# Split weight tiles of the projections placed 64 bytes lower in SBUF

## The chip, the cores and the metric

The kernel runs on one core of one Trainium2 chip. The metric is the time of one execution on the device in microseconds, given as the median of several runs. The kernel before takes 1052.99 us (three runs, 1051.14 to 1053.38). A profile is one further execution, taken with the hardware profiler.

## What is computed

One encoder block over T = 1040 positions (16 meta tokens and 1024 of the sequence) with a model width of 1024. A normalised input goes through one wide projection; its parts feed a bidirectional retention branch (4 heads) and a windowed attention branch (8 query heads, 2 key groups); both are gated, projected, merged and projected again. Cut to what matters here:

```python
u = _rms_norm(h, pre_w)
z = u @ w_in
rq, rk, rv, rg, aq, ak, av, ag, gr, ga = _split_in(z)
...
o_r = _bidirectional_retention(rq, rk, rv, lg_f, lg_b)[:, META_PAD:]
y_r = (groupnorm(o_r) * ret_nw * silu(rg)) @ w_rb
o_a = _windowed_sink_attention(aq, ak, av, sink)[:, META_PAD:].reshape(B, T, ATT_Q)
y_a = (o_a * silu(ag)) @ w_ab
mix = sigmoid(gr) * y_r + sigmoid(ga) * y_a
return h + _rms_norm(mix @ w_o, post_w)
```

All of it is float32. The kernel splits each factor of a large product into a high and a low half and sums three matmuls for one product.

## The kernel before

**The product of halves.** `mm3` (line 74) issues three matmuls into one PSUM bank: high by high (line 76), low of the first factor by high of the second (line 77), high by low (line 78). The first argument is the stationary operand, which TensorE loads (128 columns, a row "PEld" in the profile), the second is the moving one, which it streams.

**The input.** `big` (line 133) holds the scaled input, high half in `big0`, low half in `big1`, as eight rows (k = 0 to 7) of 48 + 1040 columns. A row has 4352 bytes, 17 times 256. Position a begins at column 48 + a, so a block that begins at position 16 begins 256 bytes into the row.

**Projections.** A unit of weights is 1024 x 256. It is fetched to two raw tiles `wr` (line 105), and `halves_w` (line 112) splits each into a high tile `wh` (GpSimd or ScalarE) and a low tile `wl` (VectorE), of 128 x 1024 values, 4096 bytes a partition. There are four buffers of each in the pool `wp` (line 48).

- `proj` (line 136) has the weights stationary (128 columns of a `wh` or `wl` tile) and a block of `big` moving: 512 positions for retention's queries (tiles `pq`) and attention's queries (`paq`); 272, 256, 256 and 256 positions for retention's and attention's keys (`pk`, `pak`; `PIECES`, line 23).
- `projT` (line 157) has a block of 128 positions of `big` stationary and 256 columns of a weight tile moving (retention's values `pv`, attention's values `pav`). For the meta tokens the stationary operand is `xm` (48 or 16 columns), also in `wp`.
- `gen_pre` (line 796) computes parts of the gates' products ahead of time (tiles `pe`): weights `weh` and `wel`, again in the buffers of `wp`, stationary, and 512 positions of `big` moving.

**Order.** First a setup with the first head's queries and keys, then four heads of retention with the next projections filled in between (`retention`, line 446), attention's values (`gen_av`, line 872), attention (`attention`, line 1360) with the query projections and the `pe` pieces filled in between, and from 555 us on the gates, the two branch projections and the output projection in a form with seven products instead of eight (class `Phase`; tiles `bz`, `br`, `ba`, `bo`; its split weights are `lh`, `ll`). The order of work on each engine comes from the order of the program, from explicit "issue after" rules, and from a planner that simulates the program while it is built.

**Where the tiles lie.** The pools `edge`, `wp`, `aw` and later `lp` stand at the upper end of SBUF and grow downwards: a pool that needs more bytes begins at a lower address, and what stands below it moves down too. `edge` holds one tile (`nsink`). When attention is over, `wp` and `aw` are closed (line 1552) and `lp` takes their place directly below `edge` (line 1553). A tile of `lp` waits for the last use of those older tiles whose bytes it overlaps. In the program before the change, in bytes of a partition:

| tiles | pool | starts | start modulo 256 |
|---|---|---|---|
| `big`, blocks from position 16 on (256 bytes into a row) | keep | 7040 + multiples of 128 columns | 128 |
| `big`, the first piece of the keys (from position 0) | keep | 6976 | 64 |
| `wh` (four) | wp | 196480, 200576, 204672, 208768 | 128 |
| `wl` (four) | wp | 212864, 216960, 221056, 225152 | 128 |
| `xm` | wp | 194944 | 128 |
| `raw0`, `raw1` | aw | 175296, 176928 | 192, 32 |
| `aqh`, `aql` (attention's split queries, four each) | aw | 178560 to 192896, every 2048 | 128 |
| `kTh`, `kTl` (attention's keys, moving, blocks of 272 columns) | ra | 98432 on | 128, 192, 0, 64 |
| `vah` (attention's values, stationary) | va | 131328 on, every 1024 | 0 |
| `pah`, `pbh`, `Sh`, `kh` and the like | ap, rp | | 0 |
| `lh`, `ll` (split weights from 555 us on) | lp | 171904 to 194432, every 2048 | 128 |
| the two raw tiles of odd units, `wrz1_0` and `wrz1_1` | lp | 196480, 200576 | 128 |

`weh13` and `wel13`, the weights of the last `pe` pieces, lie in the buffers at 204672 and 221056; `weh11` lies at 200576.

The lines that the change touches: the two loops at line 273 in which the first `wh` and `wl` tiles are made, and `split_q` (line 645), which splits a block of attention's queries into `aqh` and `aql`.

Of the kernel before, what the change touches and what calls it, by code (L numbers as in the profile page):

```python
# [7 lines left out]
F32 = mybir.dt.float32  # L8
# [8 lines left out]
P = 128  # L17
# [22 lines left out]
def block_kernel(ctx: ExitStack, tc: tile.TileContext, x0, xT, x, meta, w_in, w_rb, w_ab, w_out, post_w,  # L40
# [7 lines left out]
    wp = w_stack.enter_context(tc.tile_pool(name="wp", bufs=1, side="right"))  # L48
# [42 lines left out]
    def dve_lo(o, i, hi):  # L91
        return nc.vector.tensor_tensor(o, i, hi.bitcast(F32), ALU.subtract).ins  # L92
# [174 lines left out]
    with tc.tile_pool(name="setup", bufs=1, reuse_waits="tile") as st:  # L267
# [6 lines left out]
        for i in range(2):  # L274
            raws.append(keep.tile([P, 4, 256], F32, tag="wr", bufs=2, name=f"wr0_{i}"))
            for j, lst in enumerate(wt):
                lst.append(wp.tile([P, 4, 256], R, tag="wl" if j else "wh", bufs=4, name=f"w0_{i}_{j}"))

        def w0_part(k0, k1):
            v = tuple(t[k0 // 4][:, k0 % 4:k0 % 4 + k1 - k0] for t in (raws, wt[0], wt[1]))  # L280
            nc.sync.dma_start(v[0], w_in[U_QK, :, k0:k1, :])
            if k0 == 4:
                nc.scalar.copy(v[1], v[0])
            else:
                raised[k0] = pool_hi(v[1], v[0])
            return lambda: dve_lo(v[2], v[0], v[1])
# [70 lines left out]
        for c in range(9):  # L357
            a, b = cols(c)
            t = st.tile([P, D if c < 7 else T], F32, tag="xn" if c < 7 else "xr", bufs=7 if c < 7 else KT - 1,
                        name=f"xn{c}")[:, 0:D]  # L360
# [282 lines left out]
    aq, aqs, wq = {}, {}, {}  # L643

    def split_q(hp, e_, i):

        o = aq[hp][e_, i]
        h, l = (aw.tile([P, 512], R, tag=f"aq{t}", bufs=4, name=f"aq{t}{hp}_{i}{e_}") for t in "hl")
        nc.scalar.copy(h, o)
        dve_lo(l, o, h)  # L650
        aqs[hp, e_, i] = h, l
# [702 lines left out]
    aw = w_stack.enter_context(tc.tile_pool(name="aw", bufs=1, reuse_waits="tile", side="right"))  # L1354
# [5 lines left out]
    def attention():  # L1360
# [4 lines left out]
        def stage1(hp, n):  # L1365
# [19 lines left out]
            for e_ in range(2):  # L1385
                hd = 2 * hp + e_
                if (hp, e_, i) not in aqs:
                    split_q(hp, e_, i)
                a_, b_ = (t[:, o0:o0 + P] for t in aqs[hp, e_, i])
                s = p2(f"ps{hd}_{n}")  # L1390
                mm3(s[:, 0:wid], a_, b_, kh[:, start:start + wid], kl[:, start:start + wid], True, True)
                if n == 0:
                    if hp:
                        raw[e_] = aw.tile([P, 401], F32, tag=f"raw{e_}", bufs=1, name=f"raw{hd}")
                    nc.vector.tensor_copy(raw[e_][:, 0:1], nsink[:, hd:hd + 1])
                p = pp[:, e_]
                nc.vector.tensor_tensor_reduce(raw[e_][:, 1:1 + wid], s[:, 0:wid], mask[0][:, mo:mo + wid], -SCALE,  # L1397
                                               nsink[:, hd:hd + 1], ALU.add, ALU.min, nm_[:, e_:e_ + 1])

                last["exp"] = nc.scalar.activation(p[:, 0:1 + wid], raw[e_][:, 0:1 + wid], AF.Exp, scale=-1.0,  # L1400
                                                   bias=nm_[:, e_:e_ + 1], accum_out=den[:, e_:e_ + 1]).ins
                pt.append(p[:, 1:401])
# [83 lines left out]
        for k, (hp, n) in enumerate(chunks):  # L1486
# [28 lines left out]
            if k in (12, 14, 21):  # L1515
# [3 lines left out]

    BEGUN = {0: [(fetch_aq, 1)], 9: [(half_w, 'q', 1, 0)], 10: [(sum_fetch, 0)], 12: [(half_w, 'q', 1, 1)],  # L1520
             14: [(pre_fetch, 7)], 17: [(split_q, 0, 0, 1)], 19: [(pre_sum, 7, 0)], 20: [(pre_sum, 7, 1)],
             21: [(split_q, 0, 1, 1)], 25: [(pre_sum, 7, 2)], 27: [(pre_parts, 7)], 28: [(pre_fetch, 8)],
             33: [(split_q, 1, 0, 0)], 34: [(sum_row, 0, 0)], 36: [(sum_row, 0, 1)], 38: [(split_q, 1, 1, 0)],
             39: [(sum_fetch, 1)], 40: [(pre_sum, 8, 0)], 41: [(pre_sum, 8, 1)], 42: [(pre_sum, 8, 2)],
# [129 lines left out]
```

## Time and profile before

| | us |
|---|---|
| median of three runs | 1052.99 |
| the profiled execution, whole | 1049.72 |
| its span, first to last instruction | 1047.6 |
| around the span | 2.12 |
| setup and the first head's queries and keys | 0 to 30 |
| retention with projections | 30 to 305 |
| attention's values | 305 to 335 |
| attention with query projections and `pe` pieces | 335 to 555 |
| gates (`bz`) | 555 to 812 |
| branch and output projections | 812 to 1047.6 |

In the profile, PE is TensorE's matmuls, PEld its loads of stationary operands, DVE is VectorE, ACT ScalarE, POOL GpSimd and SP the queue that issues most DMAs; "SPq" is such an issue. L76 is line 76. A row of matmuls gives the tiles as out<-moving,stationary or out<-stationary,moving with the buffer numbers left out, then the stationary and the moving shape. Matmuls overlap: the time from one start to the next is shorter than the duration of one, and where nothing stops them the two move together: a matmul that lasts some ns longer starts its successor as many ns later.

### The profile page before, as it was taken

The page shows a single profiled execution, that of the slowest core. Times are in us where ns is not written, and L with a number is a line of the kernel's source. Part 1 is how long each engine was busy: PE and PEld are TensorE (multiplying, and loading weights), DVE is VectorE, ACT ScalarE, POOL GpSimd, SP SyncE. Part 2 cuts the span into 40 slices and gives each one's busy share as a digit, 9 for nine tenths or more (in the row PEclk, how much of TensorE's full clock was granted, in tenths as well). Part 3 has the DMA queues.
Part 4 walks back from the last instruction along what each step waited for, and adds up shares of the span by engine and source line. Part 5 has one row for each costly group of instructions (what it writes and reads, how often), then busy time and mean ns, then how long its engine had stood idle before and what let it go on. Part 6 is the DMA issues. An engine that isn't in the chain of part 4 may idle for free. (4 is left out here: it accounts for less than half of the span.)

```text
span 1047.6 us, 17241 instructions
## 1 busy us (share of the span) xinstructions
PE 1032.9 (99%) x5880; PEld 906.8 (87%) x5880; DVE 838.9 (80%) x1788; ACT 505.6 (48%) x1127; POOL 227.1 (22%) x338
## 2 busy tenths in 40 slices
PE   8999999999999999999999999999999999999997
PEld 7998999989989888988888888787888788788886
DVE  6876768758876787777778988998899899877665
ACT  5541332522423557665667545455457446334443
POOL 3444244243342423443410000000000000111032
PEclk9999999999999999999999999999999999999999
DMA  9433123233341457665649579999935746789464
GB/s 352 165 85 88 61 45 88 75 71 109 82 99 62 100 153 200 182 168 136 186 153 350 193 255 333 298 328 348 379 131 169 242 171 217 233 224 330 131 121 80
DMA packets 98838, 188.43 MB, mean 180 GB/s; under 512 B 13024, under 2 KB 37632, under 8 KB 98192
## 3 DMA queue, kind: packets, MB, share of 16 engines
q1 hardware_dynamic: 81200, 162.89, 46.5%
q0 software_dynamic: 10176, 14.73, 9.4%
q10 hardware_dynamic: 7376, 9.73, 2.6%
q8 instruction: 46, 0.75, 0.3%
q14 instruction: 40, 0.33, 0.1%
HBM read 124.32 MB, written 57.68 MB: 174 GB/s over the span
## 5 line engine op out<-in xcount | busy, mean ns | idle before, releaser
L1269 POOL DMA_DIRECT2D mx_d<-c1a x4 | 3.6, 888 | 395.2 <-DVE c1a L1260 395.2
L77 PE MATMUL bz<-big,llz 128*128 128x512 f32 x192 | 74.8, 390 | 0.1
L76 PE MATMUL bz<-big,lhz 128*128 128x512 f32 x192 | 74.1, 390 | 0.5 <-ACT lhz L956 0.5
L78 PE MATMUL bz<-big,lhz 128*128 128x512 f32 x192 | 74.2, 389 | 0.0
L76 PE MATMUL pv<-wh,big 128*128 128x256 f32 x256 | 73.6, 288 | 0.0
L77 PE MATMUL pv<-wh,big 128*128 128x256 f32 x256 | 73.5, 287 | 0.0
L78 PE MATMUL pv<-wl,big 128*128 128x256 f32 x256 | 73.5, 287 | 0.0
L77 PE MATMUL bz<-T,llz 128*128 128x512 f32 x176 | 68.6, 390 | 1.1 <-DVE llz L92 1.1
L78 PE MATMUL bz<-T,lhz 128*128 128x512 f32 x176 | 68.5, 389 | 0.0
L76 PE MATMUL bz<-T,lhz 128*128 128x512 f32 x176 | 68.0, 389 | 0.0
L1400 ACT ACTIVATE p<-raw,nm 128x401 f32<-128x401 f32 (+1 forms) x64 | 38.3, 600 | 34.3 <-DVE nm L1397 33.0
L1410 POOL TENSOR_SCALAR p<-p,den 128x400 f32<-128x400 f32 (+1 forms) x60 | 37.7, 684 | 67.8 <-DVE den L1403 65.9
L76 PE MATMUL paq<-big,wh 128*128 128x512 f32 x128 | 51.4, 402 | 0.0
L77 PE MATMUL paq<-big,wl 128*128 128x512 f32 x128 | 50.0, 391 | 0.1
L78 PE MATMUL paq<-big,wh 128*128 128x512 f32 x128 | 50.1, 392 | 0.0
L76 PEld LDWEIGHTS pv<-wh,big 128*128 128x128 f32 x256 | 48.8, 191 | 0.4
L77 PEld LDWEIGHTS pv<-wh,big 128*128 128x128 f32 x256 | 48.8, 191 | 0.4
L78 PEld LDWEIGHTS pv<-wl,big 128*128 128x128 f32 x256 | 48.8, 191 | 0.3
L92 DVE TENSOR_TENSOR wl<-wr,wh 128x1024 fp32r<-128x1024 f32 x28 | 35.0, 1254 | 11.7 <-POOL wh L89 6.6
L76 PEld LDWEIGHTS bz<-big,lhz 128*128 128x128 f32 x192 | 36.0, 188 | 8.6 <-ACT lhz L956 1.3
L77 PEld LDWEIGHTS bz<-big,llz 128*128 128x128 f32 x192 | 36.0, 188 | 7.9 <-DVE llz L92 0.5
L78 PEld LDWEIGHTS bz<-big,lhz 128*128 128x128 f32 x192 | 36.0, 188 | 7.5
(616 smaller groups left out, 3598.5 us busy)
## 6 DMA issues: line engine op xcount, KB each, us to landing
wrz<-in_w_in_dram SPq DMA_DIRECT2D x32, 512.0 KB, 6.0
wr<-in_w_in_dram SPq DMA_DIRECT2D x29, 512.0 KB, 4.1
we<-in_w_in_dram SPq DMA_DIRECT2D x16, 512.0 KB, 4.3
tg<-tg_d SPq DMA_DIRECT2D x32, 256.0 KB, 5.1
e<-e ACTq DMA_DIRECT2D x20, 256.0 KB, 2.6
e<-e SPq DMA_DIRECT2D x20, 256.0 KB, 4.7
xn<-in_x_dram SPq DMA_DIRECT2D x8, 512.0 KB, 9.8
oTr_d<-ost SPq DMA_DIRECT2D x16, 256.0 KB, 2.1
```

Of the source, the lines that this page charges most:

```text
L76: nc.tensor.matmul(o, ah, bh, start=first, stop=False, **kw)
L77: nc.tensor.matmul(o, al, bh, start=False, stop=False, **kw)
L78: latest[:] = [nc.tensor.matmul(o, ah, bl, start=False, stop=last, **kw).ins]
L92: return nc.vector.tensor_tensor(o, i, hi.bitcast(F32), ALU.subtract).ins
L1269: nc.gpsimd.dma_start(d, to, accum_op=ALU.add)
L1400: last["exp"] = nc.scalar.activation(p[:, 0:1 + wid], raw[e_][:, 0:1 + wid], AF.Exp, scale=-1.0, bias=nm_[:, e_:e_ + 1], accum_out=den[:, ...
L1410: nc.gpsimd.tensor_scalar(pt[e_][:, 0:wid], pt[e_][:, 0:wid], den[:, e_:e_ + 1], 1.0, op0=ALU.mult, op1=ALU.mult)
```

## The change

Two tiles are allocated and never written or read: 64 bytes a partition in `wp`, after the first weight tiles, and 192 bytes in `aw`, after the first two query tiles. No instruction is added or removed.

```diff
@@ -275,6 +275,7 @@
             raws.append(keep.tile([P, 4, 256], F32, tag="wr", bufs=2, name=f"wr0_{i}"))
             for j, lst in enumerate(wt):
                 lst.append(wp.tile([P, 4, 256], R, tag="wl" if j else "wh", bufs=4, name=f"w0_{i}_{j}"))
+        wp.tile([P, 16], F32, name="space_w")
 
         def w0_part(k0, k1):
             v = tuple(t[k0 // 4][:, k0 % 4:k0 % 4 + k1 - k0] for t in (raws, wt[0], wt[1]))
@@ -646,6 +647,8 @@
 
         o = aq[hp][e_, i]
         h, l = (aw.tile([P, 512], R, tag=f"aq{t}", bufs=4, name=f"aq{t}{hp}_{i}{e_}") for t in "hl")
+        if not aqs:
+            aw.tile([P, 48], F32, name="space_aq")
         nc.scalar.copy(h, o)
         dve_lo(l, o, h)
         aqs[hp, e_, i] = h, l
```

With the two tiles at the upper ends of their pools, `xm`, `wh` and `wl` begin 64 bytes lower, at 64 modulo 256. The pool `aw` begins 64 + 192 = 256 bytes lower, so `raw0`, `raw1`, `aqh` and `aql` keep their place modulo 256. Everything else, `lp` included, keeps its address. Since `lp` stays and `wp` moves down, a tile of `lp` that ended where a tile of `wp` began now overlaps its first 64 bytes.

## The prediction

> **What bounds the kernel now.** I read the page's busy table first, then the same table by stretches of time.
>
> ```profile
> span 1047.6 us, 17241 instructions
> PE 1032.9 (99%) x5880; PEld 906.8 (87%) x5880; DVE 838.9 (80%) x1788; ACT 505.6 (48%) x1127; POOL 227.1 (22%) x338
> ...
> 30.00:85.00 55.00, 55.00 (x435) 53.38 (x433) 42.03 (x109) 22.48 (x62) 23.04 (x29) 1.00 0.32 94
> 335.00:555.00 220.00, 218.73 (x1292) 194.48 (x1290) 166.68 (x416) 134.98 (x354) 73.14 (x126) 1.00 0.58 161
> 555.00:806.00 251.00, 249.25 (x1100) 205.24 (x1100) 232.64 (x384) 141.32 (x252) 0.00 (x0) 1.00 0.81 279
> ...
> PE pq L76 <- ACT big L330: 1.6, 2, 1.1
> ```
>
> In a row of stretches stand the length, then busy time and count of PE, PEld, DVE, ACT and POOL. PE is busy in 55.00 of 55.00 us and in 218.73 of 220.00; the longest sum of waits of PE on any one line is 1.6 us (last row, from the list of waits). So the kernel is a train of matmuls without gaps, and the time is their number times their distance. The chain that ended last covers 0.4% of the span and says nothing more. What the change can do to the time it must do through the distance between matmuls that read a moved tile, or through a new wait that makes a gap.
>
> So the next view is the duration of such matmuls, by tile (minimum/median/maximum in ns) and by group (busy us, mean ns).
>
> ```profile
> L78 PE MATMUL bz<-big,lhz 128*128 128x512 f32 x192 | 74.2, 389 | 0.0
> L78 PE MATMUL paq<-big,wh 128*128 128x512 f32 x128 | 50.1, 392 | 0.0
> L77 PE MATMUL paq<-big,wl 128*128 128x512 f32 x128 | 50.0, 391 | 0.1
> L78 PE MATMUL pe<-big,weh 128*128 128x512 f32 x80 | 31.3, 392 | 0.0
> L78 PE MATMUL pq<-big,wh 128*128 128x512 f32 x48 | 18.7, 390 | 0.0
> ...
> L78 PE MATMUL paq<-big,wh x128: 387/389/398, 293.3 to 504.1; 128*128 128x512 f32 x128
> L77 PE MATMUL pq<-big,w x16: 389/395/398, 5.7 to 27.0; 128*128 128x512 f32 x16
> ```
>
> A matmul of 512 columns has a settled duration, 389 ns: it is the median everywhere, and the mean too in the gates, where one follows the other undisturbed. And it has an unsettled one, around 395: the median in the setup, where matmuls of 512, 272 and 256 columns alternate. The projections between retention and attention pieces lie between, at 390 to 392. The cause of the unsettled ones shows where a row of settled matmuls ends.
>
> ```profile
> L78 PE MATMUL paq<-big,wh x3: 389/389/396, 436.6 to 438.0; 128*128 128x512 f32 x3
> 437.96 0.40 PE L78 MATMUL paq<-big,wh 128*128 128x512 f32 x1
> 438.20 0.28 PE L76 MATMUL po<-pah,vah 128*128 128x256 f32 x1
> ...
> L78 PE MATMUL paq<-big,wh x2: 389/389/389, 442.7 to 443.4; 128*128 128x512 f32 x2
> 443.42 0.39 PE L78 MATMUL paq<-big,wh 128*128 128x512 f32 x1
> 443.64 0.28 PE L76 MATMUL pak<-big,wh 128*128 128x256 f32 x1
> ```
>
> Both are the last of a settled row, and both are followed by one of 256 columns, whose stationary operand is loaded while they stream. At 437.96 that operand is `vah`, which begins at 0 modulo 256, and the matmul takes 396 ns; at 443.42 it is a `wh` tile, at 128 like the block of `big` that streams, and it takes 389. So what the next load reads seems to matter to a stream by some 7 ns, and the place modulo 256 is what I see differ. All 512-wide work in this kernel has both at 128. The change takes that equality away from all projections.
>
> **The change part by part.** Nothing is removed or issued anew; three things move.
>
> *(a) The 512-wide projections* (`pq`, `paq`, `pe`): stationary at 64, moving at 128. By the counts, (128 + 80 + 48) x 3 = 768 matmuls; the 48 of the setup, unsettled already, are not in it. The trace has no 512-wide stream beside a load 64 bytes off, so I bound it: from below by the fastest of the row of `paq`, 387 ns, from above by the slowest, 398. Against the present mean of about 391.5 (392, 391, 392, 390 in the rows above) that is -3.5 to +5 us over 768. I take 395, the unsettled median: 768 x 3.5 ns = +2.7 us.
>
> *(b) The 256-wide ones* (`pv`, `pav`, `pk`, `pak`). Here the weights are moving at 64 and `big` stationary at 128, or the reverse.
>
> ```profile
> L78 PE MATMUL pk<-big,wh 128*128 128x256 f32 x72 | 20.3, 282 | 0.0
> L78 PE MATMUL pk<-big,wh 128*128 128x272 f32 x24 | 6.9, 288 | 0.0
> L78 PE MATMUL pv<-wl,big x256: 277/283/385, 31.0 to 275.8; 128*128 128x256 f32 x128
> L78 PE MATMUL pav<-wl,big x64: 279/283/364, 308.4 to 334.9; 128*128 128x256 f32 x64
> L78 PE MATMUL pak<-big,wh 128*128 128x256 f32 x48 | 13.5, 282 | 0.0
> L76 PE MATMUL pb<-Shb,qh 128*128 128x256 f32 x4 | 1.1, 280 | 0.0
> L77 PE MATMUL pb<-Shb,ql 128*128 128x256 f32 x4 | 1.1, 281 | 0.0
> ```
>
> There are (256 + 64 + 72 + 48) x 3 = 1320. Their settled duration is 283 ns, and the unsettled one is the shorter: `pb` (groups of a window, 85 to 108 us), three matmuls at a time between other work, has 280 to 281. The 272-wide pieces of the keys are the only long rows that have the two operands 64 bytes apart already (moving at 64, stationary at 128). Between 283 ns at 256 columns and 389 at 512 a column costs (389 - 283) / 256 = 0.41 ns, so 272 settled ones would take 289.6; they take 288. Both rows say 1.5 to 2.5 ns less. Bounds: from 278 (near the minima, 277 and 279) to 285 (the mean of L76 of `pk`, stalls included) against 283, so -6.6 to +2.6 us. I take -1.5 ns: 1320 x 1.5 = -2.0 us.
>
> ```profile
> L76 PE MATMUL pk<-big,wh 128*128 128x256 f32 x72 | 20.5, 285 | 0.0
> ```
>
> The 272-wide ones, (24 + 16) x 3 + 24 = 144, get both operands to 64 and may settle: +1.6 ns each, +0.2 us. The meta matmuls (stationary `xm`, moving `wh`, both in `wp`) keep their distance: nothing.
>
> *(c) The new overlap in `lp`.* Of the tiles that overlap 64 bytes of a further weight tile, one meets a late one: `wrz1_1` now ends inside `weh13`, and its load has to wait for the last `pe` matmul. Three others that matter early (`wrz1_0`, `llz1_1`, the first `xT`) get `weh11`, `weh10` and `wel11`, whose pieces come before those of `weh13` and are through when the first of these loads is issued.
>
> ```profile
> 544.96 4.35 SPq L1200 DMA_DIRECT2D wrz<-in_w_in_dram  x4
> 549.36 16.26 SPq L1120 DMA_DIRECT2D xT<-xs  x15
> ...
> 553.38 0.69 DVE L994 TENSOR_TENSOR stz0S<-wrz,wrz 128x512 f32<-128x512 f32 x1 [3.30 <-PE pe L78]
> 558.47 0.68 DVE L994 TENSOR_TENSOR stz1S<-wrz,wrz 128x512 f32<-128x512 f32 x1
> DMA to landing us min/median/max: 3.7/5.3/6.7
> ...
> 554.93 0.40 PE L76 MATMUL bz<-big,lhz 128*128 128x512 f32 x1
> 558.77 0.62 ACT L932 CAST big<-xT 128x512 fp32r<-128x512 f32 x1
> 563.88 0.68 DVE L92 TENSOR_TENSOR llz<-stz1S,lhz 128x512 fp32r<-128x512 f32 x1
> 564.39 0.84 PE L76 MATMUL bz<-big,lhz 128*128 128x512 f32 x3
> ```
>
> The four loads `wrz` are issued from 544.96 to 549.31, `wrz1_1` last. The last `pe` matmul ends at 553.38, where DVE is released. So the load is issued some 4.4 us later, and the fifteen `xT` loads behind it on SP's queue with it. With the landing times of the third row from the end of that block (3.7 to 6.7 us) it is there at 557.1 to 560.1; its first reader is DVE at 558.47, so DVE comes 0 to 1.6 us late, and everything queued behind that instruction on DVE with it, up to the split of 563.88 that the matmuls of 564.39 want. The three L76 in one row there show that PE takes the high parts first because the low one is just being made: there is little slack. The `xT` loads are first read at 558.77 by ACT; issued at 553.8 they may come as late, but PE needs those products only after 570 us: six others of 12 matmuls come first, from 554.93 on, at some 0.227 us a matmul, the 0.22 to 0.24 us between the starts in the rows at 438 and 443. Bounds 0 to +1.6 us; DVE's other splits can go on meanwhile, so I take +0.5. The planner may put another load in front instead; the same bounds hold.
>
> *(d) The splits themselves.*
>
> ```profile
> L92 DVE TENSOR_TENSOR wl<-wr,wh x28: 1186/1224/1660, 24.7 to 465.8; 128x1024 fp32r<-128x1024 f32 x28
> ```
>
> DVE now reads `wr` at 128 and `wh` at 64. The work stands beside PE's full stretches above and is prepared well ahead; if one took 16 ns more, 28 would be 0.4 us on an engine that is not the bound. Zero. Attention's queries keep their place: zero.
>
> The sum: 2.7 - 2.0 + 0.2 + 0.5 = +1.4 us. Made against the profiled execution, 1049.72 becomes 1051.1; the runs shown stand 3.3 us above it, so 1052.99 becomes 1054.4.
>
> The Trainium skill speaks against (a) and (b): "TensorE: Matmul & The Clock Gate", Part 2, Step-by-step, says that TensorE has two independent SBUF read ports, one for the streaming operand and one for the load, and that a load takes no read bandwidth from the running matmul. By it (a) and (b) would be nothing and the sum +0.5 us. The rows of 437.96 and 443.42 (396 against 389 ns) do not agree with it to the last 7 ns, so I give it a rival's place only (the third below).
>
> **The rivals.**
>
> *Only the 512-wide pay (slower).* One mechanism: stream and load collide in every matmul as at 437.96, and the 256-wide ones stay at 283 because they find another settled rhythm. Price: (397 - 391.5) x 768 = +4.2, with (c) +4.7 us: 1057.7. It decides from a 512-wide mean of about 394.5 on, where (a) alone passes 2.1 us. For it: the step to 396 with a load 128 bytes off. Against it: the 272-wide rows, 64 bytes off, are not slow.
>
> *The collisions get fewer (faster).* If 64 bytes between the two is better than none, as the 272-wide rows hint, the 256-wide gain 3 ns (283 to 280, the `pb` row) and the 512-wide lose their restarts (391.5 to 389.5): -4.0 - 1.5 + 0.5 = -5.0 us at best; I put it at -3.5: 1049.5. Against it: at 512 columns the unsettled state is the longer one.
>
> *Places don't matter to TensorE.* The 7 ns come from something else that differs between `po` and `pak`. For it: the skill's rule, and the score matmuls, whose moving operand begins at 0, 64 or 128 bytes from the stationary one with no row standing out. Then only (c) is left: 1053.5.
>
> ```profile
> L76 PE MATMUL ps<-kTh,aqh 128*128 128x400 f32 x48 | 16.6, 345 | 0.0
> L77 PE MATMUL ps<-kTh,aql 128*128 128x400 f32 x48 | 16.5, 344 | 0.0
> ```
>
> **How the numbers follow.** Forecast 0.34, only the 512-wide 0.29, fewer collisions 0.21, no influence 0.16. A measurement of this kernel tells about 0.2% (2.1 us) from no change. The forecast's own range is 1052.5 to 1056.5; it is slower by more than 2.1 us in four cases of ten. Slower: 0.14 + 0.28 + 0.01 = 0.43; faster: 0.19 from the third case and 0.02 from the others; the same: 0.36. The range reaches from the faster case to somewhat above the slower one, 1049.3 to 1059; the ends where all bounds of (a) and (b) meet are left out.
>
> **What would show it.** (a): medians of `paq`, `pe` and `pq` at 394 to 397 instead of 389, with `bz` still at 389. (b): medians of `pv`, `pav`, `pk` at 280 to 282. The 272-wide at 289 to 290. (c): the fourth `wrz` load issued after 553 us and a gap of PE below 1.6 us near 564. The forecast is wrong if the 512-wide rows stay at 389, if the 256-wide go above 284, or if the time moves by more than PE's durations and the gap of (c) add up to.

## The result, and the profile after

The changed kernel takes 1047.56 us (median of 8 runs, 1046.44 to 1050.19), the kernel before beside it 1051.82 us (8 runs, 1050.68 to 1053.38). The ratio is 0.9965, with a 95% interval of 0.9956 to 0.9974: faster by 0.35%, where 1054.4 us was forecast and the range ended at 1049.3 us. The profiled execution took 1046.49 us against 1049.72, so the pair of traces below shows 3.2 us of the 4.3 us between the medians; the rest can't be traced in them.

First the page of the changed kernel: span and busy times.

```profile
span 1044.4 us, 17239 instructions
PE 1029.6 (99%) x5880; PEld 902.3 (86%) x5880; DVE 838.4 (80%) x1788; ACT 506.2 (48%) x1127; POOL 227.8 (22%) x338
```

The span is 3.2 us shorter and PE is busy for 3.3 us less (1032.9 before) with the same 5880 matmuls; PE's idle time stands as before, at 14.8 us against 14.7. So no wait went away: the matmuls themselves stand closer. Which ones shows in the busy time of one tile's matmuls over the whole span. In such a row stand the stretch, its length, PE's busy time and matmul count, PEld's, then the engines that read the tile; the last three numbers are the clock, the DMA share and GB/s. Overlapping matmuls are counted once, so in a row without gaps this is the count times the distance from start to start. The kernel before, in the order `pv`, `pav`, `pk`, `pak`, `paq`, `pe`, `pq`, `bz`:

```profile
0.00:1060.00 1060.00, 117.58 (x832) 104.78 (x832) 14.76 (x36) 13.24 (x36) 1.00 0.58 178
0.00:1060.00 1060.00, 27.71 (x208) 25.60 (x208) 4.21 (x9) 4.16 (x9) 1.00 0.58 178
0.00:1060.00 1060.00, 55.18 (x384) 50.99 (x384) 14.27 (x36) 1.00 0.58 178
0.00:1060.00 1060.00, 27.20 (x192) 24.73 (x192) 6.21 (x16) 1.00 0.58 178
0.00:1060.00 1060.00, 93.86 (x384) 70.42 (x384) 20.57 (x32) 1.00 0.58 178
0.00:1060.00 1060.00, 58.77 (x240) 44.13 (x240) 11.68 (x20) 1.00 0.58 178
0.00:1060.00 1060.00, 48.24 (x192) 34.50 (x192) 11.81 (x18) 1.00 0.58 178
0.00:1060.00 1060.00, 252.40 (x1104) 206.77 (x1104) 42.04 (x62) 23.36 (x40) 1.00 0.58 178
```

The changed kernel, the same tiles in the same order:

```profile
0.00:1060.00 1060.00, 114.99 (x832) 102.59 (x832) 14.77 (x36) 13.27 (x36) 1.00 0.58 178
0.00:1060.00 1060.00, 26.79 (x208) 24.79 (x208) 4.21 (x9) 4.17 (x9) 1.00 0.58 178
0.00:1060.00 1060.00, 54.80 (x384) 50.60 (x384) 14.28 (x36) 1.00 0.58 178
0.00:1060.00 1060.00, 26.89 (x192) 24.43 (x192) 6.18 (x16) 1.00 0.58 178
0.00:1060.00 1060.00, 94.18 (x384) 70.42 (x384) 20.56 (x32) 1.00 0.58 178
0.00:1060.00 1060.00, 58.98 (x240) 44.12 (x240) 11.66 (x20) 1.00 0.58 178
0.00:1060.00 1060.00, 48.35 (x192) 34.43 (x192) 11.81 (x18) 1.00 0.58 178
0.00:1060.00 1060.00, 253.02 (x1104) 206.75 (x1104) 42.06 (x62) 23.32 (x40) 1.00 0.58 178
```

Where the weights stream (`pv`, `pav`) PE is busy 2.59 + 0.92 us less; where they are loaded and 256 or 272 columns of `big` stream (`pk`, `pak`) 0.38 + 0.31 us less; where 512 columns of `big` stream (`paq`, `pe`, `pq`) 0.32 + 0.21 + 0.11 us more. Together that is -4.20 + 0.64 = -3.56 us. The gates take 0.62 us more, though none of their operands moved and their distance from start to start is 226.8 ns in both kernels. A second profile of the changed kernel (from its repeated run, the last but one of the experiments) has 252.67 us there, 0.27 us more than before, so part of it is scatter; the experiment on the overlap returns to the rest.

The durations by tile (minimum/median/maximum in ns) of the changed kernel:

```profile
L78 PE MATMUL pv<-wl,big x256: 275/278/384, 30.7 to 272.7; 128*128 128x256 f32 x128
L78 PE MATMUL pav<-wl,big x64: 276/276/367, 305.2 to 330.8; 128*128 128x256 f32 x64
L78 PE MATMUL paq<-big,wh x128: 388/394/405, 290.1 to 499.6; 128*128 128x512 f32 x128
L78 PE MATMUL bz<-big,lhz x192: 389/389/397, 551.3 to 808.7; 128*128 128x512 f32 x192
```

The medians of `pv` and `pav` fell from 283 to 278 and 276 ns. That of `paq` in this row (L78) rose from 389 to 394, as step (a) said it would, and yet `paq` costs only 0.32 us more: a median of durations does not say how far apart the starts are, and 393 was its mean where 392 was before.

### The profile page after: what moved, and what is told of

Same layout as the page of the kernel before. It is cut to its first block, busy times and chain, and to the rows that moved or that the text cites. A ratio compares the mean times of both kernels' runs of the same rounds, so it can differ in the third digit from the quotient of the medians.

```text
span 1044.4 us, 17239 instructions
## 1 busy us (share of the span) xinstructions
PE 1029.6 (99%) x5880; PEld 902.3 (86%) x5880; DVE 838.4 (80%) x1788; ACT 506.2 (48%) x1127; POOL 227.8 (22%) x338
## 5 line engine op out<-in xcount | busy, mean ns | idle before, releaser
L77 PE MATMUL bz<-big,llz 128*128 128x512 f32 x192 | 74.8, 390 | 0.1
L78 PE MATMUL bz<-big,lhz 128*128 128x512 f32 x192 | 74.2, 389 | 0.0
L77 PE MATMUL pv<-wh,big 128*128 128x256 f32 x256 | 72.7, 284 | 0.0
L78 PE MATMUL pv<-wl,big 128*128 128x256 f32 x256 | 72.6, 284 | 0.0
L77 PE MATMUL bz<-T,llz 128*128 128x512 f32 x176 | 68.6, 390 | 0.5 <-DVE llz L92 0.5
L78 PE MATMUL bz<-T,lhz 128*128 128x512 f32 x176 | 68.5, 389 | 0.0
L78 PE MATMUL paq<-big,wh 128*128 128x512 f32 x128 | 50.3, 393 | 0.0
L77 PE MATMUL paq<-big,wl 128*128 128x512 f32 x128 | 50.2, 392 | 0.1
L77 PEld LDWEIGHTS pv<-wh,big 128*128 128x128 f32 x256 | 48.2, 188 | 0.4
L78 PEld LDWEIGHTS pv<-wl,big 128*128 128x128 f32 x256 | 48.3, 188 | 0.3
L77 PEld LDWEIGHTS bz<-big,llz 128*128 128x128 f32 x192 | 36.0, 188 | 7.9 <-DVE llz L92 0.5
L78 PEld LDWEIGHTS bz<-big,lhz 128*128 128x128 f32 x192 | 36.0, 188 | 7.5
```

The source lines that it names most:

```text
L77: nc.tensor.matmul(o, al, bh, start=False, stop=False, **kw)
L78: latest[:] = [nc.tensor.matmul(o, ah, bl, start=False, stop=last, **kw).ins]
```

## The experiments

In all of them "distance" is the place of the streamed operand minus that of the operand loaded beside it, modulo 256. In the changed kernel it is -64 for `pv` and `pav` (weights stream at 64, `big` is loaded at 128) and +64 for `pk`, `pak`, `paq`, `pe` and `pq` (`big` streams at 128, weights are loaded at 64). Each ratio is against the kernel before in runs on the same chip, whose median was 1051.0 to 1051.4 us.

### The distance: four places of the weights

Queries moved along with the weights (the tile in `aw` left out):

```diff
-        if not aqs:
-            aw.tile([P, 48], F32, name="space_aq")
```

> Weights at 64 modulo 256 as in the changed kernel, but attention's queries are not kept: aqh and aql begin at 64 too. Theory (the distance modulo 256 between the operand that streams and the one that is loaded beside it sets a matmul's duration): only the score matmuls ps change their distances, and they come three at a time; at most 0.3 us either way, 1047.3 to 1048.0. Rival (the queries have to stay at 128): the ps rows rise from 344 or 345 ns to 348 or more, at least +0.5 us and some more through longer restarts behind them, 1048.5 to 1050.

Measured: 1047.28 us, ratio 0.9967 (0.9954 to 0.9979). That is the changed kernel: keeping the queries at 128 plays no part in it.

Weights at 0, 128 bytes from `big`:

```diff
-        wp.tile([P, 16], F32, name="space_w")
+        wp.tile([P, 32], F32, name="space_w")
-            aw.tile([P, 48], F32, name="space_aq")
+            aw.tile([P, 32], F32, name="space_aq")
```

> Weights at 0 modulo 256, 128 bytes from the blocks of big; queries still at 128. Theory of the distance: the 512-wide projections stay at 394 to 397 ns as in the one matmul at 437.96 of the kernel before, some +2 us against the changed kernel; the 256-wide ones lie anywhere between 277 and 283. Time 1048.5 to 1052. Rival (an odd multiple of 64 bytes as the tiles' own place is what helps): 0 is as 128, pv and pav back at 283 and the 512-wide at 389, 1051.8 as before.

Measured: 1053.0 us, ratio 1.002 (1.001 to 1.0029).

Weights at 192, which exchanges the two signs:

```diff
-        wp.tile([P, 16], F32, name="space_w")
+        wp.tile([P, 48], F32, name="space_w")
-            aw.tile([P, 48], F32, name="space_aq")
+            aw.tile([P, 16], F32, name="space_aq")
```

> Weights at 192 modulo 256, again 64 bytes from big, on the other side; queries at 128. Theory of the distance with a sign: what pv and pav gained (weights streaming, 64 before big) now goes to pk and pak (big streaming, 64 before the weights), and pv and pav get what pk and pak had: pv and pav near 281 ns, pk and pak near 278 or 279; since pv and pav are 960 of the 1320, about 1 to 1.5 us slower than the changed kernel, 1048.5 to 1049.5. Rival (own place, odd multiple of 64): as the changed kernel in every row, 1047.6.

Measured: 1051.63 us, ratio 1.0007 (0.9994 to 1.002).

Weights a full 256 bytes lower, at 128 again, as a control on everything else that moves with the pool:

```diff
-        wp.tile([P, 16], F32, name="space_w")
+        wp.tile([P, 64], F32, name="space_w")
-        if not aqs:
-            aw.tile([P, 48], F32, name="space_aq")
```

> Weights 256 bytes lower, so at 128 modulo 256 again, queries too; the pools move further than in the changed kernel, and wrz1_1 overlaps weh13 by 256 bytes. Theory of the distance: every row of the projections as before the change (512-wide 389, 256-wide 283, paq L78 392), 1051.8. Rival (any move of the pool, or the new overlap in lp, made the gain): as the changed kernel, 1047.6.

Measured: 1051.17 us, ratio 1.0 (0.9988 to 1.0012).

The control's rows of busy time, `pv` and `paq`:

```profile
0.00:1060.00 1060.00, 117.59 (x832) 104.80 (x832) 14.81 (x36) 13.24 (x36) 1.00 0.59 178
0.00:1060.00 1060.00, 93.90 (x384) 70.42 (x384) 20.58 (x32) 1.00 0.59 178
```

The same with the weights at 0:

```profile
0.00:1060.00 1060.00, 117.03 (x832) 104.18 (x832) 14.84 (x36) 13.24 (x36) 1.00 0.59 178
0.00:1060.00 1060.00, 95.24 (x384) 70.56 (x384) 20.58 (x32) 1.00 0.59 178
```

And with the weights at 192, `pv`, `pk` and `paq`:

```profile
0.00:1060.00 1060.00, 116.27 (x832) 103.56 (x832) 14.81 (x36) 13.24 (x36) 1.00 0.59 178
0.00:1060.00 1060.00, 54.18 (x384) 50.21 (x384) 14.29 (x36) 1.00 0.59 178
0.00:1060.00 1060.00, 95.47 (x384) 70.43 (x384) 20.58 (x32) 1.00 0.59 178
```

A move by 256 changes nothing: to 0.04 us the rows of `pv` and `paq` are those of before. So the place modulo 256 decides, and not the order of the tiles or the overlaps. At 128 bytes the 512-wide pay (`paq` +1.38 us) and the 256-wide gain little (`pv` -0.55). At 192 the signs are exchanged, and so are the gains: `pk`, now at -64, gains 1.00 us where the changed kernel gave it 0.38, `pv`, now at +64, gains 1.31 instead of 2.59, and `paq`, now at -64, pays 1.61 instead of 0.32. The whole comes out at no change that the runs can tell. Both times missed what was expected: 1053.0 us against 1048.5 to 1052 with the weights at 0, and 1051.63 us against 1048.5 to 1049.5 at 192, where only the 256-wide matmuls had been thought to exchange their gains and the price of the 512-wide at -64 was left out.

### Distance or place: both operands moved

Weights at 192 and everything on the left side of SBUF, `big` among it, 64 bytes higher, at 192 too:

```diff
-    mhalf = keep.tile([P, 40], F32, name="mhalf")
+    mhalf = keep.tile([P, 56], F32, name="mhalf")
-        wp.tile([P, 16], F32, name="space_w")
+        wp.tile([P, 48], F32, name="space_w")
-            aw.tile([P, 48], F32, name="space_aq")
+            aw.tile([P, 16], F32, name="space_aq")
```

> Weights at 192 modulo 256 as in the third experiment, and everything on the left side of SBUF 64 bytes higher, so that big stands at 192 too. The stream and the loads of the projections are then at distance 0 as before the change; in the gates, branches and output (2100 matmuls of 512 columns) the stream stands 64 bytes above the loaded operand, which keeps 128. Theory of the signed distance: pv back at 119.2 ns from start to start, pk at 119.3, paq and pe at 228.7; bz, br, ba, bo +0.8 ns on 226.7, that is +1.7 us; in all 1053. Rival, the weights' own place: pv 117.4, pk 115.4, paq and pe 233 as in the third experiment, the gates unchanged: 1051.6.

Measured: 1052.21 us, ratio 1.0011 (1.0002 to 1.002). `pv`, `paq` and `bz`:

```profile
0.00:1060.00 1060.00, 117.59 (x832) 104.79 (x832) 14.81 (x36) 13.28 (x36) 1.00 0.59 178
0.00:1060.00 1060.00, 93.89 (x384) 70.43 (x384) 20.58 (x32) 1.00 0.59 178
0.00:1060.00 1060.00, 254.54 (x1104) 207.04 (x1104) 42.49 (x62) 23.39 (x40) 1.00 0.59 178
```

Weights left where the change put them (64), and the left side 64 bytes lower, so that `big` stands at 64:

```diff
-    mhalf = keep.tile([P, 40], F32, name="mhalf")
+    mhalf = keep.tile([P, 24], F32, name="mhalf")
```

> The changed kernel (weights at 64 modulo 256) with everything on the left side of SBUF 64 bytes lower, so that big stands at 64 as well: distance 0 in the projections, and in the 2100 matmuls of the gates, branches and output the stream 64 bytes below the loaded operand. Theory of the signed distance (third experiment: 512-wide 233 ns with the stream 64 below): pv, pav at 119.2, paq, pe at 228.7, and bz, br, ba, bo up to 4 to 6 ns longer than 226.7, that is +8 to +13 us: 1060 to 1065. Rival, the weights' own place: pv 115.7 as in the changed kernel, gates 226.7, time 1047.6. Rival, distance without sign: gates +0.8 ns, 1053.

Measured: 1058.77 us, ratio 1.0071 (1.0055 to 1.0087). `pv`, `paq` and `bz`:

```profile
0.00:1060.00 1060.00, 117.58 (x832) 104.78 (x832) 14.82 (x36) 13.28 (x36) 1.00 0.59 178
0.00:1060.00 1060.00, 93.93 (x384) 70.42 (x384) 20.58 (x32) 1.00 0.59 178
0.00:1060.00 1060.00, 259.17 (x1104) 207.25 (x1104) 42.53 (x62) 23.40 (x40) 1.00 0.59 178
```

Its page:

```profile
span 1056.2 us, 17239 instructions
PE 1044.5 (99%) x5880; PEld 907.0 (86%) x5880; DVE 838.6 (79%) x1788; ACT 507.2 (48%) x1127; POOL 228.9 (22%) x338
```

In both kernels the weights are moved and the distance is 0, and `pv` and `paq` are back at 117.6 and 93.9 us, the rows of before. The weights' own place is thereby ruled out. The gates, which the change left alone, now feel it: at +64 `bz` is busy for 2.14 us more than before, at -64 for 6.77 us more. The sizes were less well foreseen. At +64 the gates' distance grew by 2.1 ns, not 0.8 (from 226.8 to 228.9, in the table below), which over 2100 matmuls would be 4.4 us, and the time rose by some 1.2 us (the ratio), with PE 3.0 us longer busy and 1.5 us less idle in the profile; at -64 it grew by 6.5 ns, and PE was busy for 11.6 us more (1044.5 against 1032.9) while the span grew by 8.6, since PE's idle time shrank from 14.7 to 11.7 us, and the 1058.77 us stay below the 1060 to 1065 expected. Where PE waited for another engine anyway, the slower matmuls first used up the wait.

### The overlap in `lp`

The changed kernel with two empty tiles in `lp`, so that no tile of it overlaps the weights of the last `pe` matmuls:

```diff
     def raw_tile(self, u, j):
+        first = u % 2 and not spaced
+        if first:
+            spaced.append(lp.tile([P, 48], F32, name="space_l"))
         t = (lp if u % 2 else keep).tile([P, 4, 256], F32, tag="wr", bufs=2, name=f"wr{self.nm}{u}_{j}")
+        if first:
+            spaced.append(lp.tile([P, 16], F32, name="space_r"))
```

> The changed kernel, with lp's tiles spaced so that no tile of lp overlaps the weights of the last pe matmuls. If the wait of the fourth wrz load cost something (the prediction's +0.5 us, 0 to 1.6), the time is that much below the changed kernel's 1047.6 and the small gaps of PE near 704 us, 1.1 us larger in the changed kernel's profile, are gone. If the wait costs nothing, the time is the changed kernel's within 1 us, ratio 0.9965 +- 0.001, and such gaps come and go with the profile.

Measured: 1047.14 us, ratio 0.9959 (0.9946 to 0.9972). The waits of SP's queue in the changed kernel between 535 and 570 us (total, times and longest in us; its line numbers are 1 higher than those of before from line 278 on, and 3 higher from line 651 on):

```profile
SPq L1203 <- DVE we L785: 6.5, 1, 6.5
SPq L1203 <- PE pe L78: 4.5, 1, 4.5
```

The same without the overlap:

```profile
SPq L1210 <- DVE we L785: 6.2, 1, 6.2
SPq L1130 <- DMA oTa_d<-oa: 4.2, 1, 4.2
```

The first sums on DVE of the first two units of the gates, in time order (start and duration in us), in the changed kernel:

```profile
548.93 0.69 DVE L997 TENSOR_TENSOR stz0S<-wrz,wrz 128x512 f32<-128x512 f32 x1 [3.31 <-PE pe L78]
554.01 0.69 DVE L997 TENSOR_TENSOR stz1S<-wrz,wrz 128x512 f32<-128x512 f32 x1
```

Without the overlap:

```profile
550.32 0.69 DVE L1004 TENSOR_TENSOR stz0S<-wrz,wrz 128x512 f32<-128x512 f32 x1 [3.32 <-PE pe L78]
555.40 0.69 DVE L1004 TENSOR_TENSOR stz1S<-wrz,wrz 128x512 f32<-128x512 f32 x1
```

PE's waits of the gates on `u2z`, first in the changed kernel:

```profile
PE bz L76 <- DVE u2z L1049: 0.9, 1, 0.9
```

Without the overlap:

```profile
PE bz L76 <- DVE u2z L1056: 0.7, 1, 0.7
```

The wait of 4.5 us that step (c) found is there in the changed kernel and gone here. In both, `stz1S`, the first reader of the late load, begins 5.08 us after `stz0S` (554.01 - 548.93, 555.40 - 550.32), and it was 5.09 before the change: the late load landed in time, and the wait costs nothing. It was close: in a second profile of the changed kernel, and in the control with the weights 256 bytes lower, which has the same wait of 4.5 us, the two starts are 5.21 us apart, so DVE came about 0.1 us late. The control takes the time of before all the same. The gap of PE behind `u2z`, which the kernel before did not show, is there without the overlap too, and at 0.5 us in the control with the weights at 128. So the overlap doesn't make it. Of the 4.45 us by which PE led the kernel before at 675 us of it (matmul by matmul, the order is the same), 3.2 were left at 728 us. The control, which has no lead there (it is 0.95 us behind at 675 us), falls back by another 0.7 us over the same stretch. So it isn't a lead that DVE takes back; whether the moved pool or the one profiled execution of the kernel before makes the difference stays open.

### Steps that are no multiple of 64

Weights 32 bytes lower than before, at 96:

```diff
-        wp.tile([P, 16], F32, name="space_w")
+        wp.tile([P, 8], F32, name="space_w")
-            aw.tile([P, 48], F32, name="space_aq")
+            aw.tile([P, 56], F32, name="space_aq")
```

> The changed kernel with half the step: weights at 96 modulo 256, 32 bytes below the place of before, the queries kept. If the place within 64 bytes does not matter and the two operands must lie a whole 64 bytes apart to be out of each other's way, some reads still meet: pv and pav between 119.2 and 115.7 ns from start to start, about 117.5, paq and pe about 229: some 1049.5. If any small step down will do, pv is at 115.7 or below and the time at 1047.5 or below. If only steps of 64 count, pv is at 119.2 and the time is that of before.

Measured: 1052.04 us, ratio 1.0008 (0.9998 to 1.0018). `pv` and `paq`:

```profile
0.00:1060.00 1060.00, 116.79 (x832) 104.00 (x832) 14.81 (x36) 13.25 (x36) 1.00 0.59 178
0.00:1060.00 1060.00, 95.51 (x384) 70.32 (x384) 20.58 (x32) 1.00 0.59 178
```

Weights 96 bytes lower, at 32:

```diff
-        wp.tile([P, 16], F32, name="space_w")
+        wp.tile([P, 24], F32, name="space_w")
-            aw.tile([P, 48], F32, name="space_aq")
+            aw.tile([P, 40], F32, name="space_aq")
```

> Weights at 32 modulo 256, 96 bytes below the place of before. Between the 64 of the change (pv 115.7, paq 229.6) and the 128 of the second experiment (pv 118.3, paq 232.5): about pv 117 and paq 231, some 1050.2, if the effect goes evenly with the distance; pv 115.7 and paq 229.6, 1047.5, if it goes in steps of 64 rounded down, pv 118.3 and paq 232.5, 1053, if rounded up.

Measured: 1052.66 us, ratio 1.002 (1.001 to 1.003). `pv` and `paq`:

```profile
0.00:1060.00 1060.00, 116.77 (x832) 103.95 (x832) 14.81 (x36) 13.25 (x36) 1.00 0.59 178
0.00:1060.00 1060.00, 95.65 (x384) 70.41 (x384) 20.58 (x32) 1.00 0.59 178
```

A step of 32 gives `pv` 0.79 of the 2.59 us, less than the half expected, and costs `paq` 1.65 us, where some 0.1 were expected. A step of 96 is for both widths about what 128 is (`pv` gains 0.81 us here and 0.55 there, `paq` pays 1.79 and 1.38), the third of the cases written down for it. But a rule of steps of 64 rounded up does not hold at 32, which would then be like 64.

What the runs give together, as the mean distance from start to start in ns, worked out from the starts in the traces (distances over 1.2 times the median of the class, the stalls, are left out):

| distance | 256-wide | 512-wide |
|---|---|---|
| 0 | `pv` 119.2, `pav` 119.5, `pk` 119.3 | `paq` 228.7, `pe` 228.7, `bz` 226.8 |
| -64 | `pv` 115.7, `pav` 114.9; `pk` 115.4 (weights at 192) | `paq` 233.1 (weights at 192), `bz` 233.3 (`big` at 64) |
| +64 | `pk` 117.8; `pv` 117.4, `pav` 117.7 (weights at 192) | `paq` 229.6, `pe` 229.5; `bz` 228.9 (`big` at 192) |
| 128 | `pv` 118.3, `pk` 118.7 | `paq` 232.5, `pe` 232.6 |
| -32 | `pv` 118.2, `pav` 118.2 | |
| +32 | `pk` 117.1 | `paq` 233.2, `pe` 233.0 |
| -96 | `pv` 118.1, `pav` 118.2 | |
| +96 | `pk` 119.1 | `paq` 233.5, `pe` 233.3 |

A mean in this table is not one spacing. At -64 a row of 256-wide matmuls keeps either to 113 to 114 ns or to 116 to 119 ns, and changes from one to the other around an interruption: of the 178 distances within `pav`'s rows in the changed kernel, 119 are of the first kind and 41 of the second; in the kernel before, 133 of 178 are 120 ns. So the mean at -64 says how often a row fell into the shorter spacing, and the distance alone doesn't settle that, as the next experiment shows.

### The other 256-wide matmuls

The changed kernel, and the same -64 for retention (`pa`, `pkv`, `pb`) and attention (`po`), by empty tiles: 64 bytes in `ra` ahead of the tag `q`, which moves attention's values (loaded) and all of retention's tiles; in `rp` 64 bytes ahead of the loaded tiles, 192 ahead of `Sh` and `Sl`, which stream, and 64 behind them; and 192 at the start of `ap`, whose tiles stream:

```diff
+                if not q:
+                    ra.tile([P, 16], F32, name="space_ra")
                 o = ra.tile([P, 512], F32, tag="q", bufs=6, name=f"qr0_{i}")
...
             vl = rp.tile([P, 256], R, tag="vl", bufs=4, name=f"vl{h}_{c}")
+            spacer("a", 16)
...
+            spacer("b", 48)
             a = rp.tile([P, 256], R, tag="Sh", bufs=2, name=f"Sh{nm}")
             b = rp.tile([P, 256], R, tag="Sl", bufs=2, name=f"Sl{nm}")
+            spacer("c", 16)
...
+    ap.tile([P, 48], F32, name="space_ap")
```

(`spacer` allocates one tile of so many values in `rp`, once for each name.)

> The changed kernel, with the same step given to the other 256-wide matmuls by empty tiles: the stream 64 bytes below the operand loaded beside it in retention (pa, pkv, pb: 456 matmuls) and attention (po, 296 less those against aq). Theory of the distance: pa, pkv, pb and po go from 118.3 to 119.0 ns to 115.0 to 116.0, some 700 x 3.3 ns = -2.3 us, 1045.3, ratio 0.9943; the projections stay as in the changed kernel. Rival, that only matmuls which follow one another in long rows, or only those with a projection's weights, gain: po, pa, pkv, pb stay at 118.3 to 119 and the time at 1047.6.

Measured: 1045.68 us (1044.84 to 1045.88), ratio 0.9945 (0.9932 to 0.9957). `po`, `pa`, `pkv`, `pb` in the changed kernel:

```profile
0.00:1060.00 1060.00, 41.04 (x296) 39.55 (x296) 11.90 (x32) 1.00 0.58 178
0.00:1060.00 1060.00, 29.54 (x192) 26.19 (x192) 15.32 (x32) 15.23 (x32) 1.00 0.58 178
0.00:1060.00 1060.00, 34.69 (x180) 26.51 (x180) 14.82 (x32) 10.24 (x28) 1.00 0.58 178
0.00:1060.00 1060.00, 14.48 (x84) 12.01 (x84) 13.44 (x28) 1.00 0.58 178
```

And here:

```profile
0.00:1060.00 1060.00, 40.60 (x296) 39.11 (x296) 11.94 (x32) 1.00 0.58 178
0.00:1060.00 1060.00, 28.99 (x192) 25.80 (x192) 15.36 (x32) 15.26 (x32) 1.00 0.58 178
0.00:1060.00 1060.00, 34.26 (x180) 26.25 (x180) 14.93 (x32) 10.20 (x28) 1.00 0.58 178
0.00:1060.00 1060.00, 14.36 (x84) 11.96 (x84) 13.47 (x28) 1.00 0.58 178
```

All four gain, 0.44 + 0.55 + 0.43 + 0.12 = 1.54 us, two thirds of the 2.3 expected: their distances went to 116.0 (`pa`) to 117.6 ns (`po`), not to 115 or 116. It is not confined to the projections' weights. The projections themselves did not all stay, though none of their operands moved. This is `pav`, which had 26.79 us in the changed kernel:

```profile
0.00:1060.00 1060.00, 27.00 (x208) 24.95 (x208) 4.22 (x9) 4.18 (x9) 1.00 0.58 178
```

Its mean distance is 116.0 ns here and 114.9 there, because 75 of the 178 distances are 113 to 114 ns instead of 119; `pk` went the other way, from 117.8 to 116.8 ns. A second profile of this kernel repeats both, so it is not scatter. What else decides between the two spacings was not tested. Since 1.5 us is near what these runs can tell, the changed kernel and this one were run once more, side by side:

> The changed kernel itself, beside the next one on the same chip: 1047.5, ratio 0.9965.

> The kernel of the seventh experiment once more, beside the changed one: 1045.7 if its gain over the changed kernel holds, 1.9 us below it, as the sum of its classes in the trace says (-1.6 us in pa, pkv, pb and po); equal to the changed kernel if the 1.9 us lay in the chance of the runs.

Measured: 1046.78 us (1046.44 to 1048.88), ratio 0.9965 (0.9953 to 0.9977), for the changed kernel, and 1045.38 us (1045.06 to 1046.35), ratio 0.9952 (0.9939 to 0.9966), for this one. The intervals of the ratios overlap, the runs do not: all ten runs of this version lie below all fourteen of the changed kernel (the closest are 1046.35 and 1046.44 us). Single runs of the two variants of the changed kernel that gain the same, with the queries moved along and without the overlap, do come as low as 1045.42 and 1045.88 us. So the further gain of some 1.4 to 1.9 us rests on the sum in the trace as much as on the times.

## Why the prediction was wrong

**The bound** was right: no gap of PE went away, and all of the gain is in the distance between matmuls that read a moved tile. That these distances depend on the places modulo 256 was right too. The direction was wrong because two terms of opposite sign were both mis-sized. Either of them put right alone would have turned the sum of +1.4 us: to -1.0 with the -4.2 us of (b), to -0.7 with the +0.64 us of (a). Both together, and nothing for (c), make the -3.56 us of the traces; the 0.7 us from there to the 4.26 us between the medians no run accounts for.

**(b), -2.0 us forecast, -4.2 us measured** (the 272-wide matmuls, +0.2 forecast, are in it). "I take -1.5 ns" was the step that failed. It was made from the 272-wide rows and from `pb`, and neither could give the price at 256 columns. The 272-wide do feel the distance, but less: the change took them from -64 to 0, and their starts moved apart by 0.7 ns (`pk`, 124.57 to 125.31) and 1.6 ns (`pak`, 124.04 to 125.68). `pb` has both operands at 0 and so told nothing of a distance. And one price was taken for both signs: 64 below is worth 3.4 to 4.6 ns (`pv`, `pav`), 64 above 1.5 to 2.7 (`pk`, and `pak` at 116.6 against 119.2; 117.4 in a second profile of the changed kernel). The bound at -6.6 us held it.

**(a), +2.7 us forecast, +0.64 us measured.** "I take 395, the unsettled median" failed in the same way. It is the median of `pq` in the setup, whose two operands both lie at 128, in between rows of other widths; so it was no price of a distance at all, and with the change it fell to 392 (L77 and L78). The starts moved apart by 0.6 to 1.0 ns, not by 3.5. "The place modulo 256 is what I see differ" was right as an observation at 437.96: of the 15 such ends of a row of `paq` before a `po`, 14 take 396 ns in the kernel before. But the load there was 128 bytes off. At 128 there is a price: `paq` +1.38 us with the weights at 0. At +64 it is 0.32. Nor does the distance to the next load set those 396 ns alone: in the changed kernel, where `big` and `vah` lie as before, 8 of the 15 take 392. The medians went to 392 to 394 (`paq`, `pq`) and 392 (`pe`), a little short of the 394 to 397 forecast, and did not bring the cost that was hung on them; the mean duration (393 against 392) did.

**(c), +0.5 us forecast, 0 measured.** The wait came, with 4.5 us on SP's queue, and the load still landed within the 5.1 us to its reader; the lower bound was the answer, and narrowly: with the reader 0.1 us late in a second profile, that it cost nothing was in part luck. **(d)** and the 272-wide (+0.15 us in the distances, +0.2 forecast) were as forecast.

**The rivals.** "The collisions get fewer" had the right sign and nearly the size for the 256-wide (3 ns); that the 512-wide would lose their restarts was wrong, they rose by 0.6 to 1.0 ns. "Only the 512-wide pay" fell with `pv`. "Places don't matter to TensorE" fell with the four places of the weights and the two kernels in which both operands moved. It was the rival by the Trainium skill, "TensorE: Matmul & The Clock Gate", Part 2, Step-by-step: two independent read ports, and a load that takes no read bandwidth from the running matmul. The runs do not agree: the same instructions take 1047.56 us with the weights at 64 and 1053.0 us with them at 0, and `bz` goes from 226.8 to 233.3 ns by a shift of 64 bytes.

What in the hardware makes the distance count is not settled. That the stream and the load beside it meet is what all the kernels are consistent with; why the sign matters, why 256 columns are best at -64 and 512 at 0, why 32 bytes are worse than +64 for the 512-wide, and what puts a row at -64 into the one spacing or the other, no run explains. A kernel with -64 for all 256-wide and 0 for all 512-wide matmuls was not tried: its weight tiles would need two places.

## What to carry to other kernels

Where TensorE streams without gaps, as here, the place modulo 256 of the streamed operand against that of the operand loaded beside it was worth up to 4% of a matmul (`pav`, 119.5 to 114.9 ns) and costs one empty tile to try; sign and width both matter, so measure each class. Read it from the busy time of one tile's matmuls over a stage without gaps, not from the median duration. A price seen at one distance (128 bytes, 396 ns) or one width (272 columns, 0.7 to 1.6 ns) is no price for another.

## What the runs showed of the hardware that was not expected

- The distance has a sign. 256-wide: 119.2 ns at 0, 115.7 at -64, 117.4 at +64 (`pv`). 512-wide: 226.8 at 0, 233.3 at -64, 228.9 at +64 (`bz`).
- Distances of 32 and 96 bytes cost a 512-wide stream as much as the worst multiple of 64 (`paq` 233.2 and 233.5 ns against 228.7).
- 64 bytes on everything on the left side of SBUF made the changed kernel 11 us slower (1058.77 against 1047.56), over two and a half times what the change had gained.
- At the same distance of -64, rows of 256-wide matmuls run at 113 to 114 ns or at 116 to 119 ns from start to start (119 and 41 of 178 in `pav`), and the shares changed to 75 and 93 when only other tiles moved.
